# Three unused pads that bring all large tiles of one core to the same place modulo 256 bytes

## The chip, the cores and the metric

The kernel runs on one core of one Trainium2 chip. A core has a matrix engine (TensorE, PE in the profile, with PEld for its weight loads), a vector engine (VectorE, DVE), a scalar engine (ScalarE, ACT), GpSimd (POOL) and a queue engine that starts most transfers (SyncE, SP). On-chip memory has 128 partitions; a tile takes the same byte range in each of its partitions, and "where a tile begins" is its byte offset within a partition. The metric is device time in microseconds (us) for one execution of the program, the median over runs.

## The reference, cut to what matters

One layer of a causal decoder on a sequence of 1024 positions and 1024 channels, all in float32:

```python
h = rms_norm(x, norm_mix_pre); z = h @ w_in                  # 1024 x 7424
z_pool, z_q, z_rwkv, z_gate = split(z)
y_pool = pool_branch(z_pool) @ w_proj_pool                   # causal means, windows 2, 4, 8, 16
y_mem  = mem_attention(z_q, mem) @ w_proj_mem                # 4 heads, 256 memory tokens
y_rwkv = rwkv_branch(shifted z_rwkv) @ w_proj_rwkv           # recurrence, 16 heads of 64
gates  = sigmoid(z_gate + gate_b)
x = x + rms_norm((gates[0]*y_pool + gates[1]*y_rwkv + gates[2]*y_mem) @ w_o)
h = rms_norm(x, norm_ffn_pre)
u = causal_dwconv(h @ w_ffn_up); u_gate, u_val = split(u)    # 1024 x 5632, three taps
x = x + rms_norm((gelu(u_gate) * u_val) @ w_ffn_down)
```

The pads touch none of this.

## The kernel before, in words

Activations are kept with channels on the partitions and positions along the free dimension, in two halves of 512 positions. Every large product is made of 128x128 weight blocks (stationary) and 128x512 pieces of activations (moving). To keep float32 accuracy in a faster format, each operand is split into a high part and a low part, both of type `fp32r`; `mm3` (lines 162 to 170) then issues three matmuls: weights high by activations high (line 167), weights high by activations low (168), weights low by activations high (169). Most of TensorE's time is these three lines. In the rows of the profile, `psg<-hh,whi` is such a matmul: result tile, then moving operand, then weights.

The stages, in order of time:

1. Input projection (`in_block`, 0 to about 1100 us). Moving operand `hh`, `hl` (the normalised input), weights `whi`, `wlo` split from `wraw`, which a DMA brings. It is interleaved with the recurrence: `rwkv_group` runs four times, each a chain of 16 steps of small matmuls (`visit`, line 639) between VectorE and ScalarE operations, and the planner puts blocks of the input projection between them (`fill_to`).
2. Attention over the memory tokens and the pooled branch (around 1000 to 1110 us), then the projections of the three branches (moving `oh`, pooled sums `ph_`/`pl_`, `yh`; from about 1107 us), and the output projection (`mgh`, `mgl`), to about 1384 us.
3. Up-projection of the feed-forward block. First plain (moving `h2h`, `h2l`; result `psg`), then from 1512 us in `up_pair`, which makes a pair of 2x2 blocked products from seven products instead of eight. Moving operands are `h2h`/`h2l` (panels B11, B21, B22, T4) or differences of them (T1, T2, T3; `t` in the rows); the weights `wt` are sums and differences, split by ScalarE and GpSimd in `parts`.
4. Down-projection (`down_pass`, from about 1850 us) in the same way, with moving operand `f` and weights `u`, both made by `step`; result `psd`. The last steps (`half_down`) overlap with the final norm and the output.

Tiles come from pools. A pool is opened on the left or on the right of the memory (`side="right"`). Left pools are stacked upwards in the order in which they are opened, right pools downwards from the top, and a closed pool's space is used by the next one opened. Inside a pool, a tag with `bufs=n` has n slots of one size, in the order in which the tags first occur. Each slot is rounded up to 32 bytes. The tile addresses of this program follow from these sizes:

| what | side | begins at, modulo 256 |
|---|---|---|
| `pv` (1320 bytes, takes 1344), first of the pool `const`, at byte 16512 | left | 128 |
| `ones`, `ident`, `bonesr`, `cent`, `mstrict`, `mincl`, `smask`, then `eps` | left | 192 |
| pool `wp` up to the `zc` slots: `st`/`xsq`/`fw`, `wraw`, `whi`, `wlo` | left | 192 |
| behind the four `zc` slots (32 bytes each): `uhi`, `ulo`, the pools `rw`, `at`, `pb`, `kvp`, `gp`, `ow`, `fa` | left | 64 |
| behind the two `mxs` slots (32 bytes each) in pool `as_`: `prb`, `pth`, `ptl` | left | 128 |
| all pools with `side="right"`: `hp`, `lr`, `pmp`, `yp`, `yq`, `hf` | right | 224 |

Between `eps` and the pool `wp` lie `inv` (64 bytes), `omu` (104, takes 128), `oka` (32) and sixteen `zc2` slots of 32 bytes: 768 bytes with `eps`, all small. The tiles named in the stages above are multiples of 512 bytes, so that pieces of them begin at the same place modulo 256 as the tile. `hh`, `hl` are in `hp`; `yh`, `yl` in `yp` and `yq`; `h2h`, `h2l` in `hf`; tags `n0` to `n15` (T3, `mgl`, four of the six places of `wt`) in `pmp`; tags `m0` to `m7` (`oh`, `ol`, `mgh`, T1, T2, `u`, `f`) in `at`; tags `q0` to `q7` (`o`, two of the six places of `wt`) in `ow`.

`parts` counts the weight tiles in `nwt` and puts them in turn in the six places:

```python
n = nwt[0] % 6
...
if n < 2:
    w = ow.tile([P, 2, 4, P], FR, name="wt", tag=f"q{n}")
else:
    w = [pmp.tile([P, 4, P], FR, name=f"wt{e}", tag=f"n{8 + (n + 1) % 4 + 4 * e}") for e in range(2)]
```

The order of the instructions on each engine is a planner's: it takes the program's order, the waits and its own estimates of durations, which don't depend on addresses. Orders that matter are pinned by hand with `later`.

Of the kernel before, what the change touches and what calls it, by code (L numbers as in the profile page):

```python
# [9 lines left out]
F32 = mybir.dt.float32  # L10
# [7 lines left out]
P = 128  # L18
# [26 lines left out]
def trunk_kernel(ctx: ExitStack, tc: tile.TileContext, xT, memT, pvec, w_in, w_kv, w_upd, w_upg,  # L45
# [4 lines left out]
    const = ctx.enter_context(tc.tile_pool(name="const", bufs=1))  # L50
    wp = ctx.enter_context(tc.tile_pool(name="wp", bufs=1))
# [22 lines left out]
    def col(name, i):  # L74
        o, w = PV[name]
        return pv[:, o + i:o + i + 1]
# [28 lines left out]
                        base=-1, channel_multiplier=-1)  # L105
    G.memset(smask, 1.0)
    G.memset(smask.rearrange("p (c s) -> p c s", s=C)[:, :, 0:1], 0.0)
    eps = const.tile([P, 3], F32, name="eps")
    for j, e in enumerate((NORM_EPS, L2_EPS, LNX_EPS)):
        G.memset(eps[:, j:j + 1], e)  # L110
# [9 lines left out]
    def split(src, hi, lo, lo_eng=None):  # L120
        A.copy(hi, src)
        return (lo_eng or V).tensor_tensor(lo, src, hi.bitcast(F32), op=ALU.subtract)
# [41 lines left out]
    def mm3(ps, w, x, start, stop):  # L164
        wh, wl = w
        xh, xl = x
        first = PE.matmul(ps, wh, xh, start=start, stop=False)  # L167
        PE.matmul(ps, wh, xl, start=False, stop=False)  # L168
        last_mm[0] = PE.matmul(ps, wl, xh, start=False, stop=stop).ins  # L169
        return first  # L170
# [27 lines left out]
    def act(dst, src, func, **kw):  # L198
        i = A.activation(dst, src, func, **kw).ins
        tc.add_manual_dep(i, phase[0].name, nosync, reason="table")  # L200
        phase[1].append(i)
# [21 lines left out]
    for k in range(KC):  # L223
        tag = ("X01", "X11", "HV", "HV")[k // 2]
# [72 lines left out]
    def in_block(j, evac, c=0, log=None):  # L297
        ws = load_w(w_in[j], KC, c=c)
        for t0, _ in HALVES:
            evac(t0, gemm(ws, hrhs(t0), log=log))  # L300

    def shifted(m, dst):

        zc = wp.tile([P, 1], F32, name="zc", tag="zc", bufs=4)

        def evac(t0, ps):
            d = dst[:, t0:t0 + 512]
            A.activation(d, ps, AF.Identity, scale=omu[:, m:m + 1])
            if t0 == 0:
                V.tensor_copy(zc, ps[:, 511:512])  # L310
            else:
                V.scalar_tensor_tensor(d[:, 0:1], zc, col("mu", m), d[:, 0:1], op0=ALU.mult,
                                       op1=ALU.add)
            V.scalar_tensor_tensor(d[:, 1:512], ps[:, 0:511], col("mu", m), d[:, 1:512],  # L314
                                   op0=ALU.mult, op1=ALU.add)
        return evac
# [49 lines left out]
    def start():  # L366
# [5 lines left out]
        kv0 = rw.tile([P, 2, T], F32, name="kv0", tag="X00")  # L372
        SP.dma_start(gr[:, 1], w_upg)
        evs = [shifted(8, kv0[:, 0]), shifted(16, kv0[:, 1])]
        for ev, ps in zip(evs, plain(0, first)):
            scaled(ev, 0, ps)
        lo_ = [(shifted(24, u), load_w(w_in[32], KC, c=0)),
               (shifted(25, gr[:, 0]), load_w(w_in[33], KC, c=1))]
        for ev, ws in lo_:
            scaled(ev, 0, gemm(ws, hrhs(0)))  # L380
# [422 lines left out]
    def pool_sums(gi):  # L803
        win = 2 << gi
        z = pb.tile([P, T], F32, name="tz", tag=f"p{gi}")
        later(SP.dma_start(z, d_zp[gi]), mem_read)
        two = [pb.tile([P, T], F32, name="ts2", tag=f"l{gi}"),
               pz.tile([P, T], F32, name="ts2", tag="ts") if gi else None]
        cur = z
        w = 1  # L810
        n = 0
        while w < win:
            nxt = two[n % 2]
            V.tensor_copy(nxt[:, 0:w], cur[:, 0:w])
            V.tensor_tensor(nxt[:, w:], cur[:, w:], cur[:, :T - w], op=ALU.add)
            cur = nxt
            w *= 2
            n += 1
        V.tensor_tensor(cur[:, 0:win], cur[:, 0:win], inv[:, 0:win], op=ALU.mult)
        V.tensor_scalar(cur[:, win:], cur[:, win:], 1.0 / win, None, op0=ALU.mult)  # L820
        V.tensor_tensor(z, cur, z, op=ALU.subtract)
        zs.append(z)

    def pool_products(gi):
        pw = load_up(w_pool[gi])
        mx = None
        for t0, _ in HALVES:
            s = slice(t0, t0 + 512)
            zh = pz.tile([P, 512], FR, name="zh", tag="zh")
            zl = pz.tile([P, 512], FR, name="zl", tag="zl")  # L830
            split(zs[gi][:, s], zh, zl, V)
            ps = gemm([pw], lambda k: (zh, zl))
            if mx is None:
                mx = pz.tile([P, T], F32, name="mx", tag="ts")
            V.tensor_scalar(mx[:, s], ps, col("pool_b", gi), col("pool_scale", gi), op0=ALU.add,
                            op1=ALU.mult)
        ph_.append(pb.tile([P, T], FR, name="ph_", tag=f"l{gi}"))
        pl_.append(pb.tile([P, T], FR, name="pl_", tag=f"p{gi}"))
        split(mx, ph_[gi], pl_[gi], V)
# [4 lines left out]
    as_ = as_ctx.enter_context(tc.tile_pool(name="as_", bufs=1))  # L844
    pool_sums(0)
    pool_sums(1)
    for hd in range(4):
        for t0, _ in HALVES:
            s = slice(t0, t0 + 512)
            q = as_.tile([P, 512], F32, name="q", tag="q", bufs=2)  # L850
            SP.dma_start(q, d_zq[hd][:, s])
            qh = as_.tile([P, 512], FR, name="qh", tag="qh")
            ql = as_.tile([P, 512], FR, name="ql", tag="ql")
            split(q, qh, ql, V)
            po = pss.tile([P, 512], F32, name="po", tag="s")
            for u in range(2):
                ps = psg.tile([P, 2, 256], F32, name="psco", tag="g0")
                for tt in range(2):
                    ts_ = slice((2 * u + tt) * P, (2 * u + tt + 1) * P)
                    mm3(ps[:, tt], (qh[:, ts_], ql[:, ts_]), (kh[:, hd], kl[:, hd]), True, True)  # L860
                mx = as_.tile([P, 8], F32, name="mxs", tag="mxs", bufs=2)
                V.reduce_max(mx[:, 0:2], ps, axis=AX.X)
                V.tensor_scalar(mx[:, 2:4], mx[:, 0:2], -SC, None, op0=ALU.mult)
                pr = as_.tile([P, 2, 256], F32, name="prb", tag="prb", bufs=2)
                for tt in range(2):
                    act(pr[:, tt], ps[:, tt], AF.Exp, bias=mx[:, 2 + tt:3 + tt], scale=SC,
                        accum_out=mx[:, 4 + tt:5 + tt])
                V.reciprocal(mx[:, 6:8], mx[:, 4:6])
                V.tensor_tensor(pr, pr, mx[:, 6:8].unsqueeze(2).broadcast_to([P, 2, 256]), op=ALU.mult)
                pt = (psc if u else psk).tile([P, 2, 2, P], F32, name="ptr", tag="c" if u else "k")  # L870
                for tt in range(2):
                    for m in range(2):
                        PE.transpose(pt[:, m, tt], pr[:, tt, m * P:(m + 1) * P], ident)
                pth = as_.tile([P, 2, 256], FR, name="pth", tag="pth", bufs=2)
                ptl = as_.tile([P, 2, 256], FR, name="ptl", tag="ptl")
                split(pt.rearrange("p m t s -> p m (t s)"), pth, ptl, V)
                for m in range(2):
                    mm3(po[:, u * 256:(u + 1) * 256], (vh[:, hd, m], vl[:, hd, m]), (pth[:, m], ptl[:, m]),
                        m == 0, m == 1)
            split(po, oh[hd][:, s], ol[hd][:, s], V)  # L880
        pool_products(hd)
        if hd < 2:
            pool_sums(hd + 2)
        for j, ev in fill[2 * hd:2 * hd + 2]:
            in_block(j, ev, 1)
# [700 lines left out]
def build(arrays):  # L1586
    import numpy as np
    import concourse.bacc as bacc

    nc = bacc.Bacc("TRN2", target_bir_lowering=False, num_devices=1)  # L1590
    aps = {n: nc.dram_tensor(f"in_{n}", a.shape, mybir.dt.from_np(a.dtype), kind="ExternalInput").ap()
           for n, a in arrays.items()}
    out = nc.dram_tensor("out_T", (D, T), F32, kind="ExternalOutput").ap()
    with tile.TileContext(nc) as tc:
        trunk_kernel(tc, **aps, out=out)
    return nc
# [10 lines left out]
```

## Time and profile before

| | |
|---|---|
| median of 3 runs | 2088.79 us (2087.73 to 2090.97) |
| span of the profiled execution, first to last instruction | 2088.0 us |
| instructions | 34125 |
| TensorE busy | 2032.2 us (97%) |
| TensorE weight loads | 1560.9 us (75%) |
| VectorE, ScalarE, GpSimd busy | 1358.1, 1070.7, 812.8 us |
| granted TensorE clock, mean | 0.995 |
| bytes moved by DMA | 221.83 MB, 106 GB/s on the mean |

The page gives no time of the profiled execution other than its span. A group's row in the profile has the line, the engine, the operation, the tiles as out<-in, the shapes and xcount, then the busy us and the mean ns of one, then the idle time of the engine ahead of them and what ended it. Matmuls overlap one another in the pipeline and their ends are modelled, so the duration of one (about 0.39 us) is longer than the distance from its start to the next one's start; the distance is what a matmul costs in an unbroken stream.

### The profile page before, as it was taken

The numbers are of one execution on the slowest core, as the hardware profiler recorded it, in microseconds if no ns is written. First come the engines' busy times: TensorE is split into PE (matmuls) and PEld (weight loads), VectorE is DVE, ScalarE is ACT, GpSimd is POOL, SyncE is SP. The second block draws the span as 40 slices with busy tenths as digits, with TensorE's granted clock in tenths as the row PEclk, the third lists the DMA queues.
The fourth block names the chain that finished last, engine by engine and source line by source line (L and its number), as shares of the span: only waits on it lengthen the run. The fifth ranks groups of instructions, "written<-read, shape, count | busy, mean of one in ns | idle before, by whom it ended". The sixth has DMA issues, their size and how long they took to land.

```text
span 2088.0 us, 34125 instructions
## 1 busy us (share of the span) xinstructions
PE 2032.2 (97%) x12246; PEld 1560.9 (75%) x12246; DVE 1358.1 (65%) x2167; ACT 1070.7 (51%) x2252; POOL 812.8 (39%) x917
## 2 busy tenths in 40 slices
PE   8999999999999999999999999998999999999997
PEld 5777767776778667876878878776788877777886
DVE  6567437654667357833695442669877777777798
ACT  7584348623773358434566243545444444444644
POOL 5521213121222121211122355565578888842341
PEclk9999999999999999999999999999999999999999
DMA  4312111120212021213526443634322222169766
GB/s 155 130 40 77 64 57 60 66 82 22 87 61 89 30 92 44 84 57 107 184 82 216 128 144 107 219 99 152 95 88 83 81 78 76 61 189 267 165 180 152
DMA packets 176713, 221.83 MB, mean 106 GB/s; under 512 B 16544, under 2 KB 128288, under 8 KB 176544
## 3 DMA queue, kind: packets, MB, share of 16 engines
q1 hardware_dynamic: 163616, 204.44, 30.1%
q0 software_dynamic: 11856, 14.16, 4.2%
q8 instruction: 97, 1.59, 0.3%
q10 hardware_dynamic: 1072, 1.05, 0.1%
q14 instruction: 72, 0.59, 0.1%
HBM read 170.30 MB, written 49.28 MB: 105 GB/s over the span
## 4 chain that ended last, share of the span: by engine, by line
PE 35%; DVE 5%; POOL 4%; DMA 4%; issue 3%; ACT 2%; SPq 1%; POOLq 0%; DVEq 0%; ACTq 0%
PE psg L167 6%; PE psg L168 6%; PE psg L169 6%; PE psf L169 2%; PE psf L168 2%; PE psf L167 2%; PE psd L168 2%; PE psd L169 2%; POOL wt L1025 2%; PE psd L167 2%; DMA R<-d_f 1%; DMA a<-in_w_fup 1%; POOL sm L1010 1%; ACT d L1041 1%; DVE d L1043 1%
## 5 line engine op out<-in xcount | busy, mean ns | idle before, releaser
L131 POOL TENSOR_TENSOR wlo<-wraw,whi 128x256 fp32r<-128x256 f32 x472 | 412.0, 882 | 955.4 <-ACT whi L128 770.0
L167 PE MATMUL psg<-hh,whi 128*128 128x512 f32 x928 | 382.7, 412 | 2.4 <-DVE kv L314 2.4
L169 PE MATMUL psg<-hh,wlo 128*128 128x512 f32 x928 | 379.4, 409 | 0.1
L168 PE MATMUL psg<-hl,whi 128*128 128x512 f32 x928 | 378.7, 408 | 0.0
L128 ACT CAST whi<-wraw 128x256 fp32r<-128x256 f32 x472 | 182.6, 403 | 231.3 <-PE psg L168 112.6
L167 PEld LDWEIGHTS psg<-hh,whi 128*128 128x128 f32 x928 | 174.4, 188 | 46.3 <-DVE kv L314 3.7
L169 PEld LDWEIGHTS psg<-hh,wlo 128*128 128x128 f32 x928 | 174.1, 188 | 46.1 <-POOL wlo L131 5.4
L168 PEld LDWEIGHTS psg<-hl,whi 128*128 128x128 f32 x928 | 174.4, 188 | 43.0 <-issue 3.6
L1025 POOL TENSOR_TENSOR wt<-a,wt 128x256 fp32r<-128x256 f32 x136 | 133.7, 1011 | 30.9 <-ACT wt L1024 30.9
L167 PE MATMUL psd<-f,u 128*128 128x512 f32 x292 | 115.2, 395 | 6.7 <-ACT f L1345 4.3
L168 PE MATMUL psd<-f,u 128*128 128x512 f32 x292 | 114.9, 394 | 0.9 <-DVE f L1349 0.9
L169 PE MATMUL psd<-f,u 128*128 128x512 f32 x292 | 114.2, 392 | 0.2 <-DVE u L1349 0.2
L1025 POOL TENSOR_TENSOR wt<-sm,wt 128x256 fp32r<-128x256 f32 x102 | 106.8, 1066 | 14.6 <-ACT wt L1024 14.6
L169 PE MATMUL psf<-h2h,wt 128*128 128x512 f32 x272 | 107.9, 397 | 0.1
L167 PE MATMUL psf<-h2h,wt 128*128 128x512 f32 x272 | 106.9, 393 | 0.1
L168 PE MATMUL psf<-h2l,wt 128*128 128x512 f32 x272 | 106.8, 393 | 0.0
L1024 ACT CAST wt<-sm 128x256 fp32r<-128x256 f32 x102 | 37.9, 404 | 128.0 <-POOL sm L1010 124.2
L1043 DVE SCALAR_TENSOR_TENSOR d<-z,pv,d 128x1023 f32<-128x1023 f32 x68 | 91.6, 1347 | 12.0 <-ACT d L1041 9.5
L169 PE MATMUL psf<-t,wt 128*128 128x512 f32 x204 | 81.5, 399 | 2.0 <-POOL wt L1025 1.9
L168 PE MATMUL psf<-t,wt 128*128 128x512 f32 x204 | 80.3, 394 | 0.0
L167 PE MATMUL psf<-t,wt 128*128 128x512 f32 x204 | 80.1, 393 | 0.0
L683 DVE TENSOR_TENSOR HV<-ph,Hd 64x128 f32<-64x128 f32 x112 | 32.3, 288 | 71.7 <-PE ph L639 47.6
(422 smaller groups left out, 4749.2 us busy)
## 6 DMA issues: line engine op xcount, KB each, us to landing
wraw<-in_w_in SPq DMA_DIRECT2D x240, 128.0 KB, 2.4
a<-in_w_fup SPq DMA_DIRECT2D x128, 128.0 KB, 2.4
d_zg<-st SPq DMA_DIRECT2D x48, 256.0 KB, 2.7
wraw<-in_w_fup SPq DMA_DIRECT2D x80, 128.0 KB, 2.4
fw<-in_w_fdn SPq DMA_DIRECT2D x33, 256.0 KB, 4.4
fraw<-d_f SPq DMA_DIRECT2D x33, 256.0 KB, 5.3
wraw<-in_w_prwkv SPq DMA_DIRECT2D x64, 128.0 KB, 2.4
wraw<-in_w_o SPq DMA_DIRECT2D x64, 128.0 KB, 2.5
```

What stands on the lines that cost most here:

```text
L128: last_whi[0] = A.copy(hi, src).ins
L131: (V if lo_on_dve[0] else G).tensor_tensor(lo, src, hi.bitcast(F32), op=ALU.subtract)
L167: first = PE.matmul(ps, wh, xh, start=start, stop=False)
L168: PE.matmul(ps, wh, xl, start=False, stop=False)
L169: last_mm[0] = PE.matmul(ps, wl, xh, start=False, stop=stop).ins
L683: ready = V.tensor_tensor(HV[q, :, c + 1, e], ph[q], Hd[q], op=ALU.add).ins
L1010: eng.tensor_tensor(out_[u], a[u], b[u], op=op)
L1024: A.copy(w[0][:, us], src[u])
L1025: last_low[0] = G.tensor_tensor(w[1][:, us], src[u], w[0][:, us].bitcast(F32), op=ALU.subtract).ins
L1041: A.activation(d, z, AF.Identity, scale=col("cw2", j), bias=col("cb", j))
L1043: V.scalar_tensor_tensor(d[:, n:], z[:, :T - n], col(cw, j), d[:, n:], op0=ALU.mult, op1=ALU.add)
```

## The change

Three edits. A tile `cpad` of 32 bytes that nothing reads or writes goes into the pool `const`, ahead of `eps`. The tag `zc`, which holds the last column of the first half of a block for `shifted`, has eight slots of one element instead of four. The tile `mxs`, whose first eight columns hold maxima and sums of the softmax, is 32 columns wide instead of 8; the other columns are not used.

```diff
@@ -105,6 +105,7 @@
     G.memset(smask.rearrange("p (c s) -> p c s", s=C)[:, :, 0:1], 0.0)
+    const.tile([P, 8], F32, name="cpad")
     eps = const.tile([P, 3], F32, name="eps")
@@ -301,7 +302,7 @@
     def shifted(m, dst):
 
-        zc = wp.tile([P, 1], F32, name="zc", tag="zc", bufs=4)
+        zc = wp.tile([P, 1], F32, name="zc", tag="zc", bufs=8)
@@ -858,7 +859,7 @@
-                mx = as_.tile([P, 8], F32, name="mxs", tag="mxs", bufs=2)
+                mx = as_.tile([P, 32], F32, name="mxs", tag="mxs", bufs=2)
                 V.reduce_max(mx[:, 0:2], ps, axis=AX.X)
```

By the sizes above, `eps` and everything behind it on the left moves by 32 bytes, what lies behind the `zc` slots by 32 + 128 = 160, and what lies behind the `mxs` slots by 160 + 192 = 352. Nothing on the right moves.

## The prediction

> **What bounds the kernel now.** I read the page's first and fifth parts, then the waits of TensorE, then windows over stretches in which TensorE does nothing but large matmuls. From the page, the span, the busy shares and the costliest matmul groups:
>
> ```profile
> span 2088.0 us, 34125 instructions
> PE 2032.2 (97%) x12246; PEld 1560.9 (75%) x12246; DVE 1358.1 (65%) x2167; ACT 1070.7 (51%) x2252; POOL 812.8 (39%) x917
> L167 PE MATMUL psg<-hh,whi 128*128 128x512 f32 x928 | 382.7, 412 | 2.4 <-DVE kv L314 2.4
> L169 PE MATMUL psg<-hh,wlo 128*128 128x512 f32 x928 | 379.4, 409 | 0.1
> L168 PE MATMUL psg<-hl,whi 128*128 128x512 f32 x928 | 378.7, 408 | 0.0
> ```
>
> TensorE is busy 97% of the span and idle for 55.8 us in all. The longest waits of TensorE (engine, line, waited for, total us, times, longest) are single events or small:
>
> ```profile
> PE psn L1094 <- DVE s L1089: 8.6, 1, 8.6
> PE px L262 <- DVE xsq L261: 5.0, 1, 5.0
> PE psf L169 <- POOL wt L1025: 1.9, 8, 0.3
> ```
>
> So nothing is gained by making TensorE wait less; only a higher rate of its 128x512 matmuls counts. The change adds no instruction that TensorE runs, so the question is whether that rate depends on where a tile begins. Windows over unbroken stretches of 128x512 matmuls (length, busy us and count for each engine, granted clock, DMA share, GB/s); the count under PEld is the number of weight loads, one for each matmul:
>
> ```profile
> core 0: us, PE busy (x) PEld busy (x) DVE busy (x) ACT busy (x) POOL busy (x), PEclk, DMA share, GB/s
> 184.31:234.48 50.17, 50.17 (x217) 40.30 (x215) 38.82 (x76) 13.11 (x30) 14.46 (x19) 1.00 0.28 93
> 1114.17:1210.39 96.22, 96.22 (x416) 77.96 (x415) 45.15 (x59) 39.92 (x74) 32.05 (x34) 1.00 0.56 180
> 1253.76:1309.39 55.63, 55.63 (x242) 44.94 (x240) 15.34 (x21) 20.57 (x50) 32.68 (x43) 1.00 0.37 112
> 1433.70:1484.58 50.88, 50.88 (x220) 40.67 (x218) 50.22 (x69) 29.48 (x64) 31.19 (x33) 1.00 0.35 107
> 1527.38:1654.24 126.86, 126.86 (x551) 103.29 (x550) 92.75 (x100) 54.60 (x116) 109.80 (x116) 1.00 0.23 76
> 1930.59:2036.24 105.65, 105.65 (x467) 87.46 (x466) 85.17 (x104) 56.90 (x101) 44.20 (x33) 1.00 0.71 173
> ```
>
> TensorE is busy without a gap in all six and its clock is full, yet a matmul takes 50.17/215 = 233.3 ns in the input projection, 231.9 and 231.8 in the branch and output projections, 50.88/218 = 233.4 in the plain up-projection, 126.86/550 = 230.7 in the up-projection by seven products, and 105.65/466 = 226.7 ns in the down-projection. Same instruction, same shape: 6.6 ns lie between first and last.
>
> **Where the tiles begin.** Worked out from the tile sizes: sizes are rounded up to 32 bytes, left-hand pools stack upwards in the order of opening, right-hand pools hang from the top. Left-hand tiles begin at 192 modulo 256 up to the `zc` tiles (weight tiles `whi`, `wlo`), at 64 behind them (`m` and `q` tags: `f`, `u`, `mgh`, `oh`, T1, T2), at 128 behind `mxs`. All right-hand tiles (`hh`, `hl`, `h2h`, `yh`, the `n` tags, T3) begin at 224. So moving operand and weights are at 224 and 192 in the input projection, at 224 or 64 and 192 in the branch and output projections, both at 64 in the down-projection. In the seven-product stage the weight tile `wt` goes round six places, two at 64 and four at 224, so both cases occur in one stage. Four products of twelve matmuls there:
>
> ```profile
> 1537.89:1540.69 2.80, 2.80 (x13) 2.26 (x12) 2.74 (x3) 1.46 (x2) 2.79 (x2) 1.00 0.26 76
> 1543.45:1546.17 2.72, 2.72 (x13) 2.25 (x12) 1.76 (x2) 1.13 (x4) 2.72 (x3) 1.00 0.17 46
> 1546.17:1548.98 2.81, 2.81 (x13) 2.26 (x12) 0.42 (x1) 0.00 (x0) 2.37 (x4) 1.00 0.60 227
> 1615.41:1618.14 2.73, 2.73 (x14) 2.25 (x12) 2.50 (x4) 0.88 (x1) 2.62 (x4) 1.00 0.23 74
> ```
>
> In this order: T2 at 64 with `wt` at 224, 233.3 ns; T3 at 224 with `wt` at 224, 226.7; B22 at 224 with `wt` at 64, 234.2; T2 at 64 with `wt` at 64, 227.5. Equal places are fast, at 64 and at 224 alike; unequal ones are slow, either way round, whatever the other engines and the DMAs do in those microseconds. Distances of 32, 128 and 160 bytes all cost much the same, so what counts is equality modulo 256.
>
> **The change part by part.** `cpad` (32 bytes) moves everything behind it on the left by 32: 192 becomes 224. Eight `zc` slots instead of four take 256 bytes instead of 128: the tiles behind them go from 64 to 224. `mxs` takes 128 bytes a slot instead of 32: what lies behind goes from 128 to 224. The right side doesn't move. Each pair of large operands becomes equal. No instruction or DMA is added, none changes its shape (`mxs` is still used in its first eight columns), nothing is queued elsewhere, no wait is added. A `zc` slot is written and last read by VectorE, which is in order, so four more slots remove no wait either. These edits cost nothing by themselves, and no cover is needed for it.
>
> What changes is the rate. The groups besides the input projection, by shape, with their counts:
>
> ```profile
> L167 PE MATMUL psg<-h2h,whi 128*128 128x512 f32 x160 | 65.3, 408 | 0.0
> L167 PE MATMUL psg<-yh,whi 128*128 128x512 f32 x128 | 50.9, 398 | 0.0
> L167 PE MATMUL psg<-mgh,whi 128*128 128x512 f32 x128 | 50.8, 397 | 1.4 <-ACT mgh L121 1.4
> L167 PE MATMUL psg<-oh,whi 128*128 128x512 f32 x64 | 25.3, 396 | 0.0
> L167 PE MATMUL psf<-h2h,wt 128*128 128x512 f32 x272 | 106.9, 393 | 0.1
> L167 PE MATMUL psf<-t,wt 128*128 128x512 f32 x204 | 80.1, 393 | 0.0
> L262 PE MATMUL px<-xsq,ones 128*128 128x512 f32 x32 | 17.0, 650 | 6.4 <-DVE xsq L261 5.0 <-ACT xsq L257 1.5
> L707 PE MATMUL pvar<-yq,bonesr 128*128 128x512 f32 x32 | 15.6, 595 | 0.0
> ```
>
> Each of lines 167 to 169 has the same count, so a row stands for three.
>
> 1. Input projection and plain up-projection: 3 x (928 + 160) = 3264. About 80% (2616) start less than 250 ns before the next large matmul; the rest stand beside small matmuls. Those 2616 go from 233.3 to 226.7: 17.3 us.
> 2. Branch and output projections: 3 x (128 + 128 + 64) = 960, and 192 more for the pooled branch by its loops (8 blocks, 2 halves, 4 tiles, 3 products). From about 232.0 to 226.7, 1152 x 5.3 = 6.1 us.
> 3. Seven-product stage: 3 x (272 + 204) = 1428 from 230.7 to 226.7: 5.7 us.
> 4. Down-projection: equal before and after, 0.
>
> Sum: 29.1 us of TensorE's time. Two parts may not reach the end. In the recurrence, TensorE alternates between a chain of small matmuls and a few large ones; one step (start, length, engine, line):
>
> ```profile
> 276.80 0.61 DVE L683 TENSOR_TENSOR HV<-ph,Hd 64x128 f32<-64x128 f32 x2 [1.30 <-ACT kv L308]
> 277.18 0.40 PE L169 MATMUL psg<-hh,wlo 128*128 128x512 f32 x1
> 277.55 0.45 PE L639 MATMUL pr<-HV,AR 128*64 128x64 f32 x8
> ```
>
> VectorE's result ends at 277.41 and the small matmul that needs it starts at 277.55, while the large one before it would have let the next begin at 277.18 + 0.23 = 277.41. So this place probably waits on VectorE, and a faster large matmul is lost there. About 420 large matmuls lie in the 60 steps (7 each), 2.8 us; I count half as lost. In the seven-product stage GpSimd is busy 109.80 of 126.86 us (87%), and it is what would be late next there; 2 of the 5.7 us I count as lost, against all or nothing as bounds. That leaves 29.1 - 1.4 - 2 = 25.7; I say 25.
>
> New inequalities: `ones` and `ident` stay at 192 while `xsq` goes to 224. The nearest rows are above: `px` with both at 192 takes 650 ns, `pvar` with 64 and 192 takes 595. Unequal isn't dearer for these f32 matmuls, so 0, with 32 x 7 ns = 0.2 us as the other end. For the other engines, two casts of one shape on ScalarE:
>
> ```profile
> L121 ACT CAST mgh<-g 128x512 fp32r<-128x512 f32 x16 | 9.9, 618 | 9.1 <-DVE g L946 9.0
> L1345 ACT CAST u<-fw 128x512 fp32r<-128x512 f32 x33 | 20.4, 620 | 32.5 <-DMA fw<-in_w_fdn 16.7 <-PE psd L169 14.1 <-issue 1.6
> ```
>
> `g` at 224 into `mgh` at 64 takes 618 ns, `fw` at 192 into `u` at 64 takes 620: no effect there; I take none on VectorE and GpSimd either.
>
> The profiled span, 2088.0, is 0.8 us under the median of the three runs, 2088.79 (2087.73 to 2090.97). **Forecast: 2088.8 - 25 = 2064 us.**
>
> **Bounds of the unknown terms.** Smallest: matched matmuls reach only 228.5 instead of 226.7 (terms 1 and 2 lose 1.8 x 3768 = 6.8), and 2.8 and 5.7 are lost whole: 29.1 - 15.3 = 14 us, 2075. Largest: the 648 others of term 1 gain 6.6 too and nothing is lost: 29.1 + 4.3 = 33, 2055.
>
> **Rivals.**
> *No change, 2089 (7%).* The rate goes with the stage and not with the place, or the pads don't bring the tiles together as I worked out. For it: the slow groups are mostly those with weights from `wraw`. Against it: the four products above, in one stage, from the same pools. The Trainium skill states the rule behind this rival, in "TensorE: Matmul & The Clock Gate", section "Step-by-step: what each phase is for": TensorE has separate read ports for the moving operand and the weights, so loading the next weights takes nothing from the running matmul. By that rule nothing would move here and the time would be 2089; the trace disagrees, 2.72 against 2.81 us for the same twelve matmuls.
>
> *The gain is given back, 2077 (7%).* Only stretches without chain or GpSimd pressure gain: term 2 (6.1) and a third of term 1 (5.8): 2088.8 - 12 = 2077. For it: the step above. Against it: between the chains TensorE runs 50 us without a gap, and its waits on GpSimd are 1.9 us in all.
>
> *Weights land later, slower (4%).* Every left tile leaves a multiple of 64 bytes. If landing there is dearer, ScalarE's casts of fresh weights are late and TensorE runs dry at the start of blocks. Landing times (count, size, median us) and ScalarE's waits on those DMAs:
>
> ```profile
> wraw<-in_w_in SPq DMA_DIRECT2D x240, 128.0 KB, 2.4
> fw<-in_w_fdn SPq DMA_DIRECT2D x33, 256.0 KB, 4.4
> R<-d_f SPq DMA_DIRECT2D x11, 256.0 KB, 7.2
> ACT whi L128 <- DMA wraw<-in_w_o: 26.7, 10, 6.1
> ACT whi L128 <- DMA wraw<-in_w_in: 23.2, 14, 3.6
> ACT whi L128 <- DMA wraw<-in_w_fup: 19.6, 8, 3.5
> ACT whi L128 <- DMA wraw<-in_w_prwkv: 12.4, 6, 3.0
> ```
>
> `fw` lands on the left in 4.4 us, `R` on the right in 7.2, 1.64 times as long. So 2.4 could become 3.9; 38 waits x 1.5 = 57 us, and 2064 + 57 = 2121. It decides from 25/38 = 0.66 us a wait. Against it: `R` and `fw` come from different sources and under different load, and TensorE has no wait for a weight DMA of its own.
>
> **How the numbers follow.** Forecast 82%, no change 7%, given back 7%, landing 4%. About 0.2% (4 us) is what a measurement of this kernel can tell from no change. Faster: forecast and given back, less a little, 0.88; same 0.07; slower 0.05. The range runs from the largest gain, 2055, to 2080, which takes in the smallest gain and most of the given-back case.
>
> **What would show it.** The stretch 184.31 to 234.48 holds 215 matmuls in 48.7 us instead of 50.2; the down-projection stays at 226.7 ns; all products of the seven-product stage take 2.72 us; the mean of the `psg<-hh` groups falls from about 410 to about 403 ns; instruction counts stay as they are. The forecast is wrong if equal tiles still run at 233 ns, if TensorE's idle time rises from 55.8 us by what its busy time loses, or if `wraw` lands later than 2.4 us.

## The result, and the profile after

The changed kernel takes 2083.97 us (median of 13 runs, 2077.21 to 2089.23) against 2090.1 us of the kernel before (13 runs, 2087.28 to 2092.08) on the same chip: a ratio of 0.9973, 95% interval 0.9963 to 0.9983. On a second chip, later, it took 2076.96 us against 2085.97, ratio 0.9962 (0.9950 to 0.9974). So it is faster by 6 to 9 us, where 25 were forecast, and 2083.97 lies outside the range of 2055 to 2080. The profiled execution took 2081.43 us, 1.9 us more than its span. The instructions stand in the same order on every engine as before; all that differs is where tiles begin.

From the page of the changed kernel, and its groups by shape (a line is one higher than before, so 168 to 170 are the three matmuls of `mm3`):

```profile
span 2079.5 us, 34125 instructions
PE 2012.2 (97%) x12246; PEld 1560.6 (75%) x12246; DVE 1355.5 (65%) x2167; ACT 1070.8 (51%) x2252; POOL 811.3 (39%) x917
L168 PE MATMUL psg<-hh,whi 128*128 128x512 f32 x928 | 379.6, 409 | 2.7 <-DVE kv L315 2.7
L170 PE MATMUL psg<-hh,wlo 128*128 128x512 f32 x928 | 376.4, 406 | 0.2
L169 PE MATMUL psg<-hl,whi 128*128 128x512 f32 x928 | 375.4, 404 | 0.0
```

TensorE's busy time fell by 20.0 us, and its idle time rose from 55.8 to 2079.5 - 2012.2 = 67.3 us: 11.5 of the 20 came back as waiting. Three waits of TensorE that grew (waited for, total us, times, longest) show where some of it went:

```profile
PE psn L1095 <- DVE s L1090: 10.1, 1, 10.1
PE psf L170 <- POOL wt L1026: 3.6, 11, 0.4
PE psg L168 <- ACT mgh L122: 3.2, 1, 3.2
```

They were 8.6, 1.9 and 1.4 us. The same six stretches as in the prediction, from the start of the same first matmul to that of the same last one (length, busy us and count of each engine, granted clock, DMA share, GB/s):

```profile
183.72:232.50 48.78, 48.78 (x217) 40.36 (x215) 38.61 (x76) 13.13 (x30) 14.00 (x19) 1.00 0.29 96
1108.58:1202.45 93.87, 93.87 (x416) 77.73 (x415) 44.99 (x59) 40.54 (x74) 31.10 (x34) 1.00 0.58 185
1246.46:1302.54 56.08, 56.08 (x242) 46.23 (x241) 15.01 (x21) 21.07 (x50) 32.63 (x43) 0.97 0.36 110
1425.65:1476.99 51.34, 50.45 (x219) 40.44 (x218) 51.26 (x70) 29.94 (x66) 31.92 (x32) 1.00 0.35 112
1519.46:1646.30 126.84, 126.40 (x551) 102.72 (x550) 93.19 (x100) 54.41 (x116) 109.75 (x116) 1.00 0.23 75
1922.01:2027.68 105.67, 105.67 (x467) 87.49 (x466) 84.86 (x104) 56.83 (x101) 44.09 (x33) 1.00 0.71 172
```

The first two gained what was forecast: 50.17 us became 48.78, and 96.22 became 93.87, 227 ns for each matmul. The third is slower than before (55.63), with a granted clock of 0.97. The fourth (50.88) and the fifth (126.86) did not gain, although their operands now begin at equal places too. The down-projection stays where it was, at 105.67 / 466 = 226.8 ns.

TensorE runs the same 12246 matmuls in the same order, so the distance from each one's start to the next one's start can be compared between two traces. The table splits it in two for each stage: distances between neighbouring large matmuls that are under 250 ns in both traces (this is the rate), and all other distances (these hold the waits and the changes between large and small matmuls). A minus is time lost. A stage runs from its first matmul to the first one of the next stage; the second profile of the changed kernel was taken on the other chip.

| stage | large neighbours under 250 ns before | forecast, us | first profile: rate, other, us | second profile: rate, other, us |
|---|---|---|---|---|
| four stretches of about 50 us without the recurrence | 845 | 5.6 | 5.5, 0.0 | 5.5, 0.0 |
| the steps of the recurrence | 167 | 1.1 | -0.2, 0.0 | -0.3, -0.1 |
| rest of the input projection | 1173 | 7.7 | 5.0, -4.6 | 4.8, -4.4 |
| plain up-projection | 458 | 3.0 | 2.8, -2.8 | 2.8, -1.7 |
| branch and output projections | 1137 | 6.1 | 6.0, -3.8 | 6.1, -1.6 |
| seven products | 1384 | 5.7 | 4.5, -4.1 | 4.4, -4.4 |
| down-projection | 840 | 0 | 0.0, 0.4 | 0.1, 0.0 |
| sum | | 29.2 | 23.6, -14.8 | 23.4, -12.2 |

The forecasts of the first four rows are the counts times 6.6 ns, together 17.4 us; the prediction's term 1 had 17.3, from a slightly different count. The sums come to 8.8 and 11.2 us; the spans differ by 8.5 and 11.3 (2079.5 and 2076.7 against 2088.0). So most of the rate came, 23.5 of 29.1 us, and half of it or more was lost again as waiting. The rate repeats within 0.3 us from profile to profile; the other column does not, since the whole input projection took 1.5 us less and 0.6 and 1.9 us more than before in profiles of three kernels below (`e3_zc_only`, `e12_sums_dve_before`, `e6_nolow_before`) that leave its places unequal.

### The profile page after: what moved, and what is told of

Its sections match the earlier page's. It is cut to its first block, busy times and chain, and to the rows that moved or that the text cites. A ratio compares the mean times of both kernels' runs of the same rounds, so it can differ in the third digit from the quotient of the medians.

```text
span 2079.5 us, 34125 instructions
## 1 busy us (share of the span) xinstructions
PE 2012.2 (97%) x12246; PEld 1560.6 (75%) x12246; DVE 1355.5 (65%) x2167; ACT 1070.8 (51%) x2252; POOL 811.3 (39%) x917
## 4 chain that ended last, share of the span: by engine, by line
PE 30%; DVE 6%; DMA 5%; POOL 5%; issue 3%; ACT 2%; SPq 1%; POOLq 0%; ACTq 0%; DVEq 0%
PE psg L168 5%; PE psg L169 5%; PE psg L170 5%; PE psf L170 3%; POOL wt L1026 3%; PE psf L168 2%; PE psf L169 2%; PE psd L169 2%; PE psd L170 2%; PE psd L168 2%; DMA a<-in_w_fup 1%; DMA R<-d_f 1%; POOL sm L1011 1%; POOL wlo L132 1%; DMA g<-d_zg 1%
```

## Experiments

**The rate by itself.** A program with nothing but large matmuls, 48 in a row for each pair of places.

```diff
+    def stretch(name, mo, wo):
+        # mo: byte offset of the moving operand; wo: byte offsets of the weights, in turn
+        ...
+        for i in range(N):
+            w0 = wo[i % len(wo)] // 4 + 128 * (i % 4)
+            m = PE.matmul(ps, wt[:, w0:w0 + 128], mv[:, mo // 4:mo // 4 + 512], start=i == 0, stop=i == N - 1)
+        ...
+    for d in (0, 16, 32, 64, 96, 128, 160, 192, 224, 240, 256, 512):
+        stretch(f"w{d}x", 0, (d,))
```

> This kernel leaves out the whole computation: it loads two blocks of x, runs unbroken streams of 48 matmuls of 128x512 in the same type, each stream with its own start of the moving operand (m) and of the weights (w) in bytes, and writes zeros and one partial product. Place theory (a matmul in a stream is slower when the moving operand and the weights loaded meanwhile begin at different places modulo 256 bytes): about 227 ns from start to start at distances 0, 256 and 512 and where both are moved by 32 or by 128; 230 to 235 ns at 32, 64, 96, 128, 160, 192 and 224. For 16 and 240 it says nothing definite, slow I think. In the stream that alternates weights at 0 and 128, every second matmul slow, mean 229 to 231. Rival (the rate goes with the stage, with the other engines or with the pools): one rate in all streams, within 1 ns.

Windows over single streams (the diff is cut); in this order, weights at +0, +16, +32, +64, +128 and +240 bytes from the moving operand's place, then both at +32, the moving operand alone at +128, both at +128, and weights alternately at +0 and +128:

```profile
19.71:30.59 10.88, 10.88 (x50) 9.01 (x48) 0.69 (x1) 0.00 (x0) 0.00 (x0) 1.00 0.01 2
30.59:41.48 10.89, 10.89 (x50) 9.01 (x49) 0.69 (x1) 0.00 (x0) 0.00 (x0) 1.00 0.00 0
41.48:52.67 11.19, 11.19 (x50) 9.02 (x48) 0.69 (x1) 0.00 (x0) 0.00 (x0) 1.00 0.00 0
52.67:63.87 11.20, 11.20 (x50) 9.02 (x48) 0.69 (x1) 0.00 (x0) 0.00 (x0) 1.00 0.01 1
75.11:86.26 11.15, 11.15 (x49) 9.04 (x48) 0.69 (x1) 0.00 (x0) 0.00 (x0) 1.00 0.01 1
119.66:130.53 10.87, 10.87 (x49) 9.01 (x48) 0.69 (x1) 0.00 (x0) 0.00 (x0) 1.00 0.00 0
163.50:174.42 10.92, 10.92 (x50) 9.01 (x48) 0.69 (x1) 0.00 (x0) 0.00 (x0) 1.00 0.01 2
174.42:185.61 11.19, 11.19 (x49) 9.01 (x48) 0.69 (x1) 0.00 (x0) 0.00 (x0) 1.00 0.00 0
185.61:196.52 10.91, 10.91 (x50) 9.01 (x48) 0.69 (x1) 0.00 (x0) 0.00 (x0) 1.00 0.00 0
196.52:207.71 11.19, 11.19 (x50) 9.12 (x48) 0.69 (x1) 0.00 (x0) 0.00 (x0) 1.00 0.01 1
```

10.88 us for 48 is 226.7 ns (+256 and +512 take 10.88 us too); 11.15 to 11.20 is 232 to 233 ns. Beside these matmuls runs only one copy on VectorE (0.69 us a window), so the effect is TensorE's own. The expectation missed in three places. Equality may be a little coarser than "modulo 256": 16 bytes to either side (+16 and +240) are as fast as +0. The stream at +192 took 229.0 ns, less than the 230 expected at least. And the alternating stream was not half slow: 11.19 us is 233 ns for each matmul, as slow as if every weight tile lay apart. The Trainium skill ("TensorE: Matmul & The Clock Gate", section "Step-by-step: what each phase is for") gives the moving operand and the weights read ports of their own; by that rule these rows would be alike, and they aren't.

**The first edit alone, and the second alone.**

Against the kernel before, the first has only this edit:

```diff
+    const.tile([P, 8], F32, name="cpad")
```

> Only the 32-byte tile in the constant pool is kept: weights of the input and plain up-projection and of the recurrent branch become equal to their moving operands (224 and 224), those of the output, pooled and memory projections stay unequal (96 and 224), the seven-product stage keeps its mixture. Theory that the rate is gained but other engines set the pace in the recurrence and in the seven-product stage: input projection at 227 to 228 ns, but only 4 to 7 us off the time, about 2085. Rival (all of the saved TensorE time reaches the end, and the loss lies only in the parts left out here): 17 + 2 us off, about 2071.

and the second only this one (the third, `mxs`, has no run of its own):

```diff
-        zc = wp.tile([P, 1], F32, name="zc", tag="zc", bufs=4)
+        zc = wp.tile([P, 1], F32, name="zc", tag="zc", bufs=8)
```

> Only the four more slots of zc are kept: tiles behind them begin at 192, as the weights do. Output, pooled and memory projections become equal (192 and 192), the input projection stays unequal (224 and 192) at 233 ns. Pace theory: 1 to 3 us off the time, 2087 to 2089, most of it between 1107 and 1200 us, where nothing paces TensorE. Rival (the equality must be at the right-hand tiles' place, or the order of instructions does it): no change of the rates, 2090.

`cpad` alone gives 2079.49 us, ratio 0.9957 (0.9944 to 0.9970), 8 us off, more than the 4 to 7 expected and far from the rival's 2071; `zc` alone 2085.77 us, 0.9990 (0.9981 to 0.9999), 2 us off, as expected. The input projection's four stretches gain 1.4 us each with `cpad`, and nothing (0.0 each) with `zc`. This one gains 2.1 us in the first stretch of the projections, where `oh` and the pooled sums meet their weights, and at most 0.9 in the stage of seven products (335.7 us against 336.6 and 336.4). So 32 bytes carry the whole measured gain. Whether the full change is even worse than `cpad` alone was then asked on one chip, since the profile of the full change has a long wait of TensorE's at 1245 us with matmuls 427 ns apart behind it, and that of `cpad` alone has not:

> The changed kernel once more, beside the next one on the same chip. Theory (its stall ahead of the output projection lasts over 3 us and is followed by matmuls at half rate, which costs what the projections gain): a second trace shows a stall over 3 us near 1245 us with about nine matmuls 427 ns apart behind it, and the median is 2082 to 2086, 2 to 5 us above the kernel with the first pad alone. Rival (that stall was an accident of one trace, and the two kernels are equally fast): no matmuls at half rate, medians within 1.5 us of one another.

> The first pad alone (the 32 bytes of `cpad`, none of the other two edits) once more. Theory: no matmuls at half rate near 1245 us, median 2079 to 2081, 2 to 5 us under the full change. Rival: within 1.5 us of the full change.

The full change took 2076.96 us (2075.82 to 2079.89), `cpad` alone 2078.22 (2076.30 to 2080.69). The two can't be told apart, so the theory's 2 to 5 us for the full change are not there, and the second profile has no matmuls at half rate at this place. Windows of 6 to 8 us around the start of the output projection, in the changed kernel's first profile and then in its second:

```profile
1243.00:1251.00 8.00, 5.38 (x15) 4.09 (x16) 1.38 (x2) 4.20 (x9) 2.80 (x4) 0.79 0.32 94
```

```profile
1243.00:1249.00 6.00, 4.09 (x17) 3.15 (x18) 1.39 (x2) 2.54 (x5) 2.33 (x3) 1.00 0.23 66
```

In the first, TensorE waited 3.2 us for `mgh` and its clock then fell (0.79 over the window): seven distances of 427 ns, with 320 and 337 at their ends, 1.6 us lost against the second, where the wait was 2.6 us and the clock stayed at 1.00. It is no accident of one trace, though. Of the six kept profiles of kernels with all three pads and the gates on SyncE's queue, five have five to seven such distances here, after waits of 1.9 to 3.2 us; of the seven other profiles of the layer none has.

**The wait for `mgh`.** TensorE now reaches the output projection earlier than ScalarE has the last gated block. In the trace ScalarE's sigmoid waits there for a gate whose load stands in SyncE's queue behind weight loads.

```diff
-            SP.dma_start(gt, d_zg[8 + j][:, s])
+            A.dma_start(gt, d_zg[8 + j][:, s])
```

> The changed kernel, with the 16 loads of the gates in the merge of the three branches started from ScalarE's queue instead of SyncE's, where they stand behind weight loads that wait for GpSimd to free a buffer; TensorE's order is the same. Theory (TensorE reaches the output projection earlier than the last gated block, which ScalarE makes late because its sigmoid waits for a gate queued behind weights): the wait of 3.6 us at 1245 us falls under 1.5 us, the nine matmuls at 427 ns behind it go back to 227, and 3 to 4 us are gained against the changed kernel (about 2080). Rival (the weights themselves land too slowly, 180 GB/s in this stretch): the wait stays over 3 us and the time within 1.5 us of the changed kernel's 2084.

2081.93 us (2078.40 to 2082.30), ratio 0.9958 (0.9944 to 0.9971). The distance between the two matmuls fell from 3.56 to 1.64 us (the wait in the rows from 3.2 to 1.3), where under 1.5 was expected, and no half-rate matmuls followed. The matmuls from 1200 to 1260 us gained 3.6 us over the first profile, but the second profile gained 2.4 of these without the edit, and 1.7 were lost in the stretch ahead, where ScalarE's order had changed. The mechanism of the wait is borne out; a gain of the whole kernel over the full change is not shown, since the ratios overlap.

**Why the recurrence gained nothing.** The prediction put it down to VectorE. The timeline of one step shows something else: in the changed kernel the large matmuls between the small ones do not run at 227 ns. Before (start, length, engine, line):

```profile
278.31 0.50 PE L167 MATMUL psg<-hh,whi 128*128 128x512 f32 x1
278.64 0.39 PE L168 MATMUL psg<-hl,whi 128*128 128x512 f32 x1
278.87 0.39 PE L169 MATMUL psg<-hh,wlo 128*128 128x512 f32 x1
279.10 0.39 PE L167 MATMUL psg<-hh,whi 128*128 128x512 f32 x1
```

After, the same step:

```profile
276.31 0.50 PE L168 MATMUL psg<-hh,whi 128*128 128x512 f32 x1
276.64 0.40 PE L169 MATMUL psg<-hl,whi 128*128 128x512 f32 x1
276.88 0.40 PE L170 MATMUL psg<-hh,wlo 128*128 128x512 f32 x1
277.11 0.40 PE L168 MATMUL psg<-hh,whi 128*128 128x512 f32 x1
```

The distances behind the first are 230 and 230 ns before, 240 and 230 after (rounded as printed; the trace has 227, 229 and 235, 234). Equal places are no faster here. That led to a program of bursts, with four small f32 matmuls ahead of each, and VectorE doing nothing but a copy or two at the end of a stream. `bursts(n, wo, count)` runs n large matmuls `count` times, with the weights `wo` bytes off:

```diff
+    for n, count in ((48, 2), (24, 4), (12, 8), (6, 12), (3, 12)):
+        bursts(n, 0, count)
+        bursts(n, 64, count)
```

> Not the layer: a program with the same kind of large matmul (128x512 moving operand, both operands of the fast type) in bursts, with four small 64x64 f32 matmuls ahead of each burst as in a step of the recurrence; it computes only products of the first two blocks of the input and writes them as the output. Bursts of 48, 24, 12, 6 and 3, each first with the operands at equal places modulo 256 bytes, then with the weights 64 bytes off. Settling theory (equal places reach 226.7 ns only after about ten matmuls in a row, since in the traces the distances behind the start of a run are 233.0, 232.7, 231.5, 230.7, 228.7 ns with equal places and 231.2, 232.2, 234.0, 233.2, 232.7 with unequal ones): the advantage of equal places per distance between neighbours is nothing in bursts of 3 (within 1.5 ns), about 1.3 ns in bursts of 6, 3.4 in bursts of 12, 4.8 in bursts of 24 and over 5.5 in bursts of 48. Rival (each matmul has its own rate, whatever came before; the recurrence keeps its time because VectorE paces it): 6.6 ns in bursts of every length.

Windows over whole streams, equal places first and then unequal: bursts of 48 (2 of them), 12 (8), 6 (12) and 3 (11 periods):

```profile
30.43:53.40 22.97, 22.97 (x116) 18.49 (x112) 0.98 (x3) 0.00 (x0) 0.00 (x0) 1.00 0.00 1
53.40:76.95 23.55, 23.55 (x116) 18.52 (x113) 0.98 (x3) 0.00 (x0) 0.00 (x0) 1.00 0.00 1
125.83:152.44 26.61, 26.61 (x164) 19.90 (x161) 0.98 (x3) 0.00 (x0) 0.00 (x0) 1.00 0.00 1
152.44:179.43 26.99, 26.99 (x164) 19.92 (x160) 0.98 (x3) 0.00 (x0) 0.00 (x0) 1.00 0.00 1
179.43:203.03 23.60, 23.60 (x173) 16.32 (x169) 0.99 (x3) 0.00 (x0) 0.00 (x0) 1.00 0.00 1
203.03:226.71 23.68, 23.68 (x172) 16.33 (x168) 0.98 (x3) 0.00 (x0) 0.00 (x0) 1.00 0.01 1
226.71:240.68 13.97, 13.97 (x125) 8.77 (x121) 0.42 (x1) 0.00 (x0) 0.00 (x0) 1.00 0.00 1
241.95:255.95 14.00, 14.00 (x125) 8.76 (x121) 0.42 (x1) 0.00 (x0) 0.00 (x0) 1.00 0.01 1
```

Per burst the advantage is 290 ns (0.58 us / 2) at 48, 48 at 12, 7 at 6 and 3 at 3; per distance 6.2, 4.3, 1.3 and about 1.4 ns (at 24: 5.4). The settling theory said over 5.5, 3.4, 1.3 and nothing within 1.5 (at 24: 4.8); the rival 6.6 everywhere, 33 ns for a burst of 6. Equal places pay in full only from the seventh distance on. In the equal stream of 12 the distances behind the first are 338, 230, 236, 228, 233, 230 and from there 227 or 226; in the unequal one 337, 235, 234, 233 and so on without an end. In the recurrence the large matmuls come one to four at a time, and no engine but TensorE is needed to explain that nothing is gained.

**The stage of seven products.** Its 1428 matmuls took, from the first to the last, before and after:

```profile
1512.43:1849.41 336.98, 334.87 (x1428) 266.23 (x1428) 249.48 (x274) 151.67 (x321) 284.82 (x295) 1.00 0.23 77
```

```profile
1504.60:1841.38 336.78, 332.92 (x1429) 264.96 (x1427) 249.50 (x273) 151.67 (x321) 284.93 (x295) 1.00 0.23 77
```

(These windows end with the last matmul's length; from start to start it is 336.59 and 336.40.) The steady distance did fall, from 230.8 to 227.6 ns. But distances above 240 ns rose from 44 to 69, and what they have above 228 ns from 7.3 to 11.7 us. The waits of TensorE's weight loads (PEld) name whom they wait for, before and after:

```profile
PEld psf L169 <- POOL wt L1025: 11.0, 24, 0.8
```

```profile
PEld psf L170 <- POOL wt L1026: 17.4, 37, 0.8
```

The weight loads wait for the low halves of `wt` that GpSimd makes, 24 times before and 37 times after; the matmuls' own rows showed only 1.9 and 3.6 us of it. GpSimd is 85% busy in both. Its groups in the changed kernel (mean ns, then its idle time and for whom it waited):

```profile
L1026 POOL TENSOR_TENSOR wt<-a,wt 128x256 fp32r<-128x256 f32 x132 | 129.8, 1011 | 30.4 <-ACT wt L1025 30.4
L1026 POOL TENSOR_TENSOR wt<-sm,wt 128x256 fp32r<-128x256 f32 x98 | 103.5, 1076 | 13.6 <-ACT wt L1025 13.6
L1011 POOL TENSOR_TENSOR sm<-sm,a 128x256 f32<-128x256 f32 x32 | 29.6, 946 | 0.0
L1011 POOL TENSOR_TENSOR sm<-a,a 128x256 f32<-128x256 f32 x32 | 24.0, 752 | 11.0 <-DMA a<-in_w_fup 8.9 <-POOL sm L1011 1.5 <-PE psf L169 0.5
```

The first attempt to relieve it gave one product's low halves to VectorE (cut to the line that asks for it):

```diff
-        V.tensor_tensor(c11, c11, prod(a12, B21), op=ALU.add)
+        V.tensor_tensor(c11, c11, prod(a12, B21, V), op=ALU.add)
```

> The changed kernel with one of the seven low halves of the weights (product of a12) computed on VectorE instead of GpSimd, 2 us less of GpSimd in each of the 17 pairs. Pace theory: GpSimd sets the pace of the seven-product stage, so this stage takes 3 to 6 us less than in the changed kernel, the whole about 2079 to 2081. Rival (the stage is paced by VectorE or by the transfers of the weights): no gain, or 2 to 5 us slower, 2084 to 2089.

2089.72 us, ratio 1.0010 (1.0001 to 1.0020): the gain of the change is gone, and the stage is 10.6 us longer:

```profile
1505.23:1852.58 347.35, 336.65 (x1429) 263.77 (x1428) 260.22 (x304) 151.63 (x321) 261.99 (x263) 1.00 0.22 74
```

GpSimd is 23 us less busy, and yet TensorE's weight loads wait 25.5 us for its low halves instead of 17.4, and only 2.2 us for those that VectorE makes. GpSimd itself now waits 65.4 us for ScalarE's casts instead of 36.2. Probably VectorE's additions come later, then ScalarE's activation that reads them (its wait for `z` rose from 33.8 to 41.7 us), then the casts behind that one; no run tested this chain. It shows that moving work off GpSimd isn't enough, and tells nothing on who paces the stage. So the low halves of the weights were left out altogether, in both kernels; the third matmul of each product uses the high half again.

```diff
-                A.copy(w[0][:, us], src[u])
-                last_low[0] = G.tensor_tensor(w[1][:, us], src[u], w[0][:, us].bitcast(F32), op=ALU.subtract).ins
-            return w
+                last_low[0] = A.copy(w[0][:, us], src[u]).ins
+            return [w[0], w[0]]
```

> The kernel before, without the low halves of the weights in the stage of seven products: the third matmul of each product uses the high half again, and the 238 subtractions of GpSimd that make the low halves are gone, so the result is less exact. Supply theory (in that stage TensorE waits for GpSimd, 87% busy, and what a faster matmul saves is given back there): the stage, from its first to its last matmul, falls from 336.6 us to about 1428 x 230.8 ns = 330 us, whole time about 2081. Rival (VectorE's additions or the transfers of the weights set that stage's time): it stays within 2 us of 336.6, whole time within 3 us of the kernel before.

> The same cut in the changed kernel. Supply theory: the stage falls from 336.4 us to about 1428 x 227.6 ns = 325 us, that is 4.5 us less than with the same cut in the kernel before, where the two kernels are 0.2 us apart with GpSimd's work in place. Rival: the stages of the two kernels stay within 1 us of one another without the low halves too.

Without the pads, and then with them:

```profile
1511.14:1844.79 333.65, 331.38 (x1429) 269.67 (x1430) 222.66 (x280) 160.43 (x325) 54.57 (x66) 0.99 0.25 84
```

```profile
1502.24:1830.41 328.17, 325.73 (x1429) 269.31 (x1430) 224.86 (x280) 160.50 (x325) 52.57 (x66) 0.99 0.26 86
```

The stages are 5.5 us apart, where they were 0.2 apart with GpSimd's work in place. Each is 3 us longer than expected: in both, one wait of 2.3 or 2.4 us for ScalarE's `wt` with six to eight matmuls 427 ns apart behind it makes nearly all of the 4.2 and 4.3 us that the distances above 240 ns have above 228. Whole times: 2074.15 and 2062.44 us, ratios 0.9932 and 0.9872, so the pads are worth 11.7 us here. The supply theory stands. Next, a relief that keeps the result: VectorE makes the two sums, which need nothing but loaded weights, and GpSimd keeps the low halves.

```diff
-        both(G, sm, a21, a22, ALU.add)
+        both(V, sm, a21, a22, ALU.add)
-        both(G, sm, sm, a11, ALU.subtract)
+        both(V, sm, sm, a11, ALU.subtract)
```

> The changed kernel with the two sums of weights that GpSimd makes in each pair of products (`sm`, four instructions of 0.74 to 0.95 us in each of 17 pairs, 52 us in the window from 1512 to 1840 us) on VectorE instead; TensorE's order is the same. Supply theory (GpSimd's work sets the time of that stage): GpSimd falls from 294 to about 240 of 355 us, the stage from 336.4 to 328 to 332 us, the whole time by 4 to 8 us. Rival (VectorE, which here takes 0.95 us for such a sum too and is in order behind additions that wait for TensorE, delivers them later than GpSimd did): the stage gets longer, as it did to 347 us when a seventh of the low halves went to VectorE.

2059.45 us (2056.06 to 2061.22), ratio 0.9873 (0.9860 to 0.9887): 17.5 us below the full change and 26.5 below the kernel before, on one chip; more than expected, and the fastest kernel of this study that computes the whole layer. Then the same edit without the pads, and both side by side:

> The kernel before (no pads) with the same two sums of each pair on VectorE. If GpSimd's work took the gain of equal places in the stage of seven products, then with that work lighter the pads are worth more: stage about 1428 x 230.8 ns = 330 us here against 324.9 with the pads, and the whole time 10 to 14 us above the next kernel, where with GpSimd's sums the pads are worth 6 to 9 us. Rival (the stage got faster for a reason of its own, and the pads add what they always add): stages within 1 us of one another, whole times 6 to 9 us apart.

> The changed kernel with these sums on VectorE, beside the kernel before with the same edit, on the same chip: 2057 to 2062 us, stage 324 to 326 us.

2071.20 us without the pads, 2059.29 with them, ratios 0.9927 (0.9913 to 0.9941) and 0.9874 (0.9861 to 0.9887). The stage without and with them:

```profile
1507.36:1837.26 329.90, 329.81 (x1430) 268.34 (x1429) 279.62 (x344) 156.45 (x325) 239.68 (x232) 1.00 0.24 82
```

```profile
1501.22:1825.85 324.63, 324.46 (x1430) 268.13 (x1430) 278.95 (x343) 154.02 (x325) 239.87 (x232) 1.00 0.24 83
```

From start to start 329.5 and 324.2 us (324.9 in the first run): 1428 x 230.8 ns = 329.6 and 1428 x 227.6 = 325.0, TensorE's own time and nothing more. The weight loads' wait for GpSimd's `wt` is down to 0.5 us. So GpSimd's supply cost the stage 7 us before the change and 11.5 to 12 after it, and took nearly all of the gain. The stage is not all that this edit changed: of the 20.0 us between the two spans (2079.5 and 2059.5), 11.5 lie in it, 2.1 in the 9 us ahead of it and 2.8 at the start of the down-projection, whose first matmul came 3.0 us after the stage's last one and now comes 0.2 us after it.

## Why the prediction was wrong

The sign and the mechanism of the rate were right, the size was not: 6 to 9 us came instead of 25. About two thirds of the miss is waiting, which the prediction put at 3.4 us and which came to 12 to 15; the rest is rate that short runs of matmuls don't reach. Step by step:

- *"Equal places are fast", 226.7 against 230 to 234 ns.* Right, and shown alone by the program of streams. *Each pair of large operands becomes equal*: right; 215 matmuls took 48.78 us, where 48.7 was said, and the down-projection stayed; the means of the three `psg<-hh` groups fell to 404 to 409 ns, less far than the 403 said. *The edits cost nothing*: nothing speaks against it; `wraw` lands in 2.3 us, `fw` in 4.2, `R` in 7.2, so the rival of later landing falls.
- *"So nothing is gained by making TensorE wait less."* This failed most. It was read off the matmuls' waits (1.9 us for `wt`) and TensorE's idle time (55.8 us). A matmul's shown length is 390 ns, though the next can start after 227: a matmul that comes up to some 160 ns late leaves no idle time in the profile. The wait stood elsewhere in the same trace: TensorE's weight loads waited 11.0 us for `wt`. The stage lost 7 us to GpSimd, and taking two sums from GpSimd brought 17.5 us on top of the change, twice what the pads did. In the whole kernel the rate brought 23.5 us of the 29.1 forecast; all other distances grew by 14.8 and 12.2 us.
- *Term 1, "those 2616 go from 233.3 to 226.7: 17.3 us".* This step failed: 5.8 and 6.5 us in the two profiles. It gave every matmul that starts less than 250 ns before the next the rate of a long stream, and short runs don't reach it: the rate came to 13.1 and 12.8 us. And outside the recurrence it put the waits at nothing; they grew by 7.3 and 6.3 us. Of these the rows name the wait for `s` (8.6 to 10.1 us, 9.0 in the second profile) and those for `HV` and `tHV` ahead of the recurrence (2.6 to 4.4 and 4.5); the rest wasn't separated, no run took it apart, and its cause stays open.
- *"So this place probably waits on VectorE", half of 2.8 us lost in the recurrence.* All of it was lost, and the reason isn't needed: bursts as short lose nearly all of the gain with VectorE idle. The 2.8 us were too many in the first place, since only 167 of these matmuls start less than 250 ns before the next large one, 1.1 us.
- *Term 2, 6.1 us.* The rate came, 6.0 and 6.1 us. What was put at nothing is the wait behind it: the one for `mgh` grew from 1.4 to 3.2 and 2.6 us, and in the first profile 1.6 us more went with the clock, so that 2.2 and 4.5 were left.
- *Term 3, 5.7 us with 2 counted as lost.* The rate brought 4.5 us, and 4.1 to 4.4 of these went as waits, so next to nothing was left. The sentence "GpSimd is what would be late next there" was right, and what failed is its price: all of it, not 2 us.
- The rival *"the gain is given back, 2077"* came nearest: it had only long, unpressed stretches gain, 12 us. Its chance of 7% was too small, above all since the 87% of GpSimd, in the prediction's own rows, spoke for it. *No change* falls with the ratios of 0.9973 and 0.9962.

## What to carry to other kernels

Put the moving operand and the weights at the same place modulo 256 bytes where TensorE runs dozens of large matmuls in a row; where it runs bursts of two to six, expect next to nothing. Before a faster rate is booked, look at the waits of the weight loads and at start-to-start distances, and not at TensorE's idle time: where a helper engine is 85% busy in the same stage, the stage's time is probably its supply. Relieve that engine first, by moving work that waits for nothing late, and the rate is worth more: 11.9 us here instead of 9.0 on the same chip.

## What the runs showed of the hardware

- The rate needs a run-up: after four small f32 matmuls, behind a first distance of 338 ns, the distances with equal places are 230, 236, 228, 233, 230 and then 227 ns, with unequal ones 233 to 235 without an end. 16 bytes of difference are harmless, 32 are not; 192 cost the least of the unequal ones (229.0 ns). Weights that lie apart every other time cost as much as weights that always do (233 ns).
- A short wait can halve TensorE's rate: distances of 427 ns follow waits for `mgh` of 3.2, 2.7, 2.2, 2.2 and 1.9 us in five profiles (the last that of the sums on VectorE, granted clock 0.76 over 7 us), but not one of 2.6 us in another. The Trainium skill ("TensorE: Matmul & The Clock Gate", section "Part 1: The HAM clock gate (the "warmup" mystery)") puts it at one idle window of about 3.4 us; the 427 ns agree with its half rate, the 1.9 us do not with that window.
- Taking 68 sums from GpSimd made an addition of VectorE's that reads two tiles faster, with the same shapes; first the changed kernel, then the one with the sums on VectorE:

```profile
L1060 DVE TENSOR_TENSOR z<-z,u 128x512 f32<-128x512 f32 x17 | 20.0, 1174 | 1.8
```

```profile
L1060 DVE TENSOR_TENSOR z<-z,u 128x512 f32<-128x512 f32 x17 | 12.6, 743 | 0.1
```

The Trainium skill ("SBUF — State Buffer", section "Who interferes with whom") has a VectorE instruction with two inputs in SBUF contend for a read port with a GpSimd instruction that reads SBUF; 1174 and 743 ns agree with that, though no run here took the port by itself.
